# Low parts of later weights behind each head's products of scores and decay, in the recurrent stage of a two-layer hybrid model

## The chip, the cores and the metric

The kernel runs on one core of one Trainium2 chip. The metric is device time in microseconds (us) of one execution: 1385.5 us as the median of three runs of the kernel before (1385.12 to 1385.57). The engines are TensorE (PE in the profile, with PEld for its weight loads), VectorE (DVE), ScalarE (ACT), GpSimd (POOL) and SyncE (SP), which issues most loads.

## What is computed

512 tokens of width 1024 go through an attention layer, a SwiGLU, a recurrent (mLSTM) layer and a second SwiGLU, each with a norm and a residual sum. The change lies in the recurrent layer:

```
def mlstm_mixer(xn, w_in, conv_w, conv_b, ig_bias, fg_bias, head_gain, w_out):
    proj = xn @ w_in
    qk = silu(causal_depthwise_conv(proj[..., :2 * QK_WIDTH], conv_w, conv_b))
    v, o_pre, gates = ...
    ig = gates[..., :MLSTM_HEADS] + ig_bias
    lf = log_sigmoid(gates[..., MLSTM_HEADS:] + fg_bias)
    h = mlstm_chunkwise(q, k, vh, ig, lf)
    h = h * rsqrt(mean(h * h, axis=-1, keepdims=True) + RMS_EPS)
    return (h * head_gain * sigmoid(o_pre)) @ w_out
```

Per head the recurrence amounts to a causal product: scores q k^T, multiplied element by element with a decay matrix exp(b_t - b_s + ig_s - m_t), the result times the values (numerators), and a quotient. There are 8 heads with 64 channels of q and k and 128 of v.

## The kernel before

**Split products.** TensorE multiplies in a rounded format. So every weight chunk (128 partitions by 1024 elements) is split in two: a high part, cast on ScalarE (L223), and a low part, the difference between the raw chunk and the high part, on VectorE (L225). Activations are split the same way. Each product is three matmuls: high weight by high activation, high weight by low activation, low weight by high activation (`multiply`, L255). In `project_tokens` (L309), where the activations are the stationary operand, the low weight comes second. Raw chunks are loaded by SyncE's queue into three buffers in turn; high and low parts have three buffers each as well.

**Chunks and ticks.** The recurrent stage projects in this order: values of heads 0 to 3, then columns of q and k and values in blocks of 256: mqk0, mqk2, mv2, mqk1, mqk3, mv3, and the output gate mo0 to mo3. Each block has two chunks. A chunk is written as: load and split of this chunk (`split_chunk`), its matmuls for two output blocks of four times three each, then `advance()`, which counts a tick and writes out the work deferred to that tick. mv2 has ticks 9 and 10, mqk1 11 and 12, mqk3 13 and 14, mv3 15 and 16, mo0 17 and 18, mo1 19 and 20, mo2 21 and 22.

**The heads.** For each head three functions are deferred to ticks given in HEAD_AT: `decay`, `scores` and `numerators`. For heads 0 to 7 the scores stand at ticks 10, 11, 13, 14, 16, 17, 19, 20.

- `decay(hh)`: one matmul broadcasts the gate row of the head into a PSUM bank (nb, L2098), VectorE adds the causal mask (L2100), ScalarE writes exponentials into four tiles e (L2105, L2108). These tiles have two buffers, so those of head h wait until the numerators of head h - 2 have been read.
- `scores(hh)`: for each of four key blocks two matmuls write a bank (L2118, L2119; two banks in turn), and one product on VectorE multiplies scores and decay into e (L2120), 512, 384, 256 and 128 columns wide.
- `numerators(hh)`: 20 matmuls (L2130) into two banks, which are then read for the denominator (L2139 to L2142), for the sum of squares on ScalarE (L2145), for a Newton root (L189 to L194) and for the scaled output (L2152). The next head's numerators need those banks. Outputs go through memory by GpSimd's queue or, for the last two heads, through TensorE.

`stack(p)` (L2083 to L2089) prepares q and k of two heads out of the convolved blocks; `convolve` (L1939 to L1943) makes these from mqk.

**What sets the order.** Instructions are written in the order above, and each engine runs its own list in a fixed order. The lists are made when the program is built: an instruction may move ahead of ones written earlier when its operands are ready sooner. Two hooks hold it back. `tc.issue_after(ins)` puts what is written inside it behind `ins` on the engine of `ins`, in order only, without a wait of its own. `behind_scores()` in `split_chunk` does this to low parts, behind the instruction kept in `ahead_of_splits[0]`; `behind_factors()` does it to the high parts, by `ahead_of_casts[0]`. The attention stage sets both; at L1338, after it, both are set to None, and in the recurrent stage nothing sets them.

## Time and profile before

| | |
|---|---|
| median of 3 runs | 1385.5 us |
| the profiled execution, its own time | 1385.26 us |
| its span | 1383.5 us |
| TensorE busy in the span | 1368.5 us |
| VectorE busy in the span | 1111.3 us |
| TensorE busy in 870 to 990 us, the heads | 117.86 of 120 us |
| VectorE busy in 870 to 990 us | 102.98 of 120 us |
| ScalarE busy in 870 to 990 us | 83.28 of 120 us |
| low parts (L225) on VectorE in 870 to 990 us | 16, 19.41 us |
| products of scores and decay (L2120) there | 32, 15.13 us |

A row of a timeline gives start, duration, engine, line, operation, what is written and read, shape and count, and in brackets the idle time of the engine before it with what ended that. A row of waits gives the waiter, who released it, the total in us, the times and the longest. A row of windows gives, for a stretch, its length and the busy time of each engine with its number of instructions, then the granted clock and the load on the DMA engines.

### The profile page before, as it was taken

The numbers are of one execution on the slowest core, as the hardware profiler recorded it, in microseconds if no ns is written. First come the engines' busy times: TensorE is split into PE (matmuls) and PEld (weight loads), VectorE is DVE, ScalarE is ACT, GpSimd is POOL, SyncE is SP. The second block draws the span as 40 slices with busy tenths as digits, with TensorE's granted clock in tenths as the row PEclk, the third lists the DMA queues.
The fourth block names the chain that finished last, engine by engine and source line by source line (L and its number), as shares of the span: only waits on it lengthen the run. The fifth ranks groups of instructions, "written<-read, shape, count | busy, mean of one in ns | idle before, by whom it ended". The sixth has DMA issues, their size and how long they took to land. (4 is left out here: it accounts for less than half of the span.)

```text
span 1383.5 us, 22546 instructions
## 1 busy us (share of the span) xinstructions
PE 1368.5 (99%) x8740; PEld 1242.9 (90%) x8740; DVE 1111.3 (80%) x1845; ACT 780.5 (56%) x1246; POOL 180.2 (13%) x264
## 2 busy tenths in 40 slices
PE   9999999999999999999999999999999999999997
PEld 7888889899998889999999998898888999999886
DVE  7758769696896489788778798898858988887887
ACT  6556565656554354444476464695534454448854
POOL 3000013121211010000010110122102330001113
PEclk9999999999999999999999999999999999999999
DMA  8534255637286256323362742324335553335863
GB/s 298 176 120 139 77 153 161 197 122 237 91 280 205 102 137 183 111 73 122 122 153 77 168 124 80 103 66 119 92 122 124 156 173 105 122 122 129 192 167 100
DMA packets 140067, 193.81 MB, mean 140 GB/s; under 512 B 8980, under 2 KB 104788, under 8 KB 139960
## 3 DMA queue, kind: packets, MB, share of 16 engines
q1 hardware_dynamic: 119552, 139.81, 31.7%
q0 software_dynamic: 18752, 51.43, 15.7%
q8 instruction: 69, 1.13, 0.3%
q10 hardware_dynamic: 1656, 1.12, 0.2%
q14 instruction: 38, 0.31, 0.1%
HBM read 167.30 MB, written 22.54 MB: 137 GB/s over the span
## 5 line engine op out<-in xcount | busy, mean ns | idle before, releaser
L1696 POOL DMA_DIRECT2D f1T<-in_ffn_w_out_dram x15 | 17.8, 1185 | 208.7 <-DMA f1P_2w_w<-in_ffn_w_out_dram 135.7
L1671 POOL DMA_DIRECT2D f0S<-in_ffn_w_out_dram x10 | 8.7, 874 | 260.3 <-DVE f0hid L1588 173.1
L2228 POOL DMA_DIRECT2D hD<-hB x32 | 21.7, 697 | 68.3 <-DVE hB L2225 68.3
L255 PE MATMUL mo<-n_h,mo_k_l 128*128 128x512 f32 x64 | 25.3, 396 | 0.0
L255 PE MATMUL mo<-n_h,mo_k_h 128*128 128x512 f32 x64 | 25.3, 395 | 0.0
L255 PE MATMUL mo<-n_l,mo_k_h 128*128 128x512 f32 x64 | 25.2, 393 | 0.0
L255 PE MATMUL awo<-ao_h,awo_k_h 128*128 128x512 f32 x64 | 25.2, 393 | 0.0
L255 PE MATMUL mqk<-n_h,mqk_k_h 128*128 128x512 f32 x64 | 25.1, 392 | 0.0
L255 PE MATMUL mwo<-yo_l,mwo_k_h 128*128 128x512 f32 x64 | 25.1, 392 | 0.0
L255 PE MATMUL mqk<-n_l,mqk_k_h 128*128 128x512 f32 x64 | 25.1, 392 | 0.0
L255 PE MATMUL f0j<-n_h,f0j_h 128*128 128x512 f32 x64 | 25.0, 391 | 0.0
L255 PE MATMUL f1j<-n_h,f1j_h 128*128 128x512 f32 x64 | 25.0, 391 | 0.0
L255 PE MATMUL awo<-ao_h,awo_k_l 128*128 128x512 f32 x64 | 25.0, 391 | 0.0
L255 PE MATMUL mwo<-yo_h,mwo_k_l 128*128 128x512 f32 x64 | 25.0, 391 | 0.0
L255 PE MATMUL mqk<-n_h,mqk_k_l 128*128 128x512 f32 x64 | 25.0, 390 | 0.0
L255 PE MATMUL awo<-ao_l,awo_k_h 128*128 128x512 f32 x64 | 25.0, 390 | 0.0
L255 PE MATMUL f0j<-n_h,f0j_l 128*128 128x512 f32 x64 | 24.9, 390 | 0.0
L255 PE MATMUL f1j<-n_h,f1j_l 128*128 128x512 f32 x64 | 24.9, 390 | 0.0
L255 PE MATMUL f0j<-n_l,f0j_h 128*128 128x512 f32 x64 | 24.9, 389 | 0.0
L255 PE MATMUL f1j<-n_l,f1j_h 128*128 128x512 f32 x64 | 24.9, 389 | 0.0
L255 PE MATMUL mwo<-yo_h,mwo_k_h 128*128 128x512 f32 x64 | 24.8, 391 | 0.0
L225 DVE TENSOR_TENSOR v1P_l<-v1W,v1P_h 128x1024 fp32r<-128x1024 f32 x14 | 17.1, 1222 | 9.3 <-ACT v1P_h L223 9.3
(2613 smaller groups left out, 5875.7 us busy)
## 6 DMA issues: line engine op xcount, KB each, us to landing
f0j_w<-in_ffn_w_in_dram SPq DMA_DIRECT2D x17, 512.0 KB, 4.8
f1j_w<-in_ffn_w_in_dram SPq DMA_DIRECT2D x17, 512.0 KB, 6.4
f1T<-in_ffn_w_out_dram POOLq DMA_DIRECT2D x15, 512.0 KB, 7.0
f0hid<-in_ffn_w_in_dram SPq DMA_DIRECT2D x9, 512.0 KB, 5.2
f1hid<-in_ffn_w_in_dram SPq DMA_DIRECT2D x9, 512.0 KB, 4.8
v0W<-in_attn_w_in_dram SPq DMA_DIRECT2D x8, 512.0 KB, 6.1
v1W<-in_attn_w_in_dram SPq DMA_DIRECT2D x8, 512.0 KB, 3.5
awo_k_w<-in_attn_w_out_dram SPq DMA_DIRECT2D x8, 512.0 KB, 4.5
```

Source lines behind the costliest of these rows:

```text
L225: nc.vector.tensor_tensor(lo[:, :n], raw[:, :n], hi[:, :n].bitcast(F32), op=ALU.subtract)
L255: nc.tensor.matmul(acc, whl[a][:, k, m * P:(m + 1) * P], pairs[b][kk], start=(kk == 0 and (a, b) == SPLITS[0]), stop=(kk == nk - 1 and (a, ...
L1671: nc.gpsimd.dma_start(t, src[1][:, ks], accum_op=ALU.add)
L1696: nc.gpsimd.dma_start(view(to), weight_rows(hk * UNITS + u, n), accum_op=ALU.add)
L2228: nc.gpsimd.dma_start(hD[k // 4].rearrange("(b i) x -> i b x", i=R)[:, :, c0:c0 + R], t[R * a_:R * (a_ + 1)])
```

## The change

One line is added in `scores`, after the loop over the four key blocks:

```
                 nc.vector.scalar_tensor_tensor(e, sp[:, :w], 0.125, e, op0=ALU.mult, op1=ALU.mult)
+            ahead_of_splits[0] = last_on(DVE) if hh < H - 1 else None
```

`last_on(DVE)` is the last VectorE instruction written so far, here the fourth product of head hh. From then on every low part written in `split_chunk` stands behind that product in VectorE's list, until the scores of the next head put their own fourth product there; the scores of head 7 take the hook away again. So the chunks written after ticks 10 to 19 are concerned: both of mqk1, mqk3, mv3, mo0 and mo1, ten low parts. High parts, loads and everything on the other engines keep their rules.

## The prediction, made before the changed kernel was run

> **What bounds the kernel now.** I read the page first, for the engine that has no room.

> ```profile
> PE 1368.5 (99%) x8740; PEld 1242.9 (90%) x8740; DVE 1111.3 (80%) x1845; ACT 780.5 (56%) x1246; POOL 180.2 (13%) x264
> PEclk9999999999999999999999999999999999999999
> ```

> TensorE is busy for 1368.5 of 1383.5 us, at a granted clock in the top tenth in every slice. A reordering on VectorE (DVE) can win only what TensorE now waits, and loses whatever new wait it makes. So the second view is TensorE's waits in the stretch of the recurrent heads, 870 to 990 us.

> ```profile
> PE m4s L2118 <- DVE m4e L2120: 0.9, 1, 0.9
> PE m6yT L351 <- DVE m6yt L2152: 0.5, 1, 0.5
> PE m1nb L2098 <- ACT m0e L2108: 0.4, 1, 0.4
> PE m6num L2130 <- DVE m5yt L2152: 0.2, 1, 0.2
> ```

> Together 2.0 us: the most that this stage can give back. The third view cuts the stretch into windows, the busy time of PE, PEld, DVE, ACT and POOL.

> ```profile
> 890.00:910.00 20.00, 20.00 (x104) 16.79 (x103) 16.20 (x39) 13.96 (x34) 1.07 (x1) 1.00 0.27 80
> 910.00:930.00 20.00, 20.00 (x149) 18.98 (x148) 19.43 (x54) 19.36 (x41) 6.45 (x8) 1.00 0.32 79
> 930.00:950.00 20.00, 18.98 (x105) 15.53 (x104) 16.78 (x56) 13.23 (x43) 7.00 (x10) 1.00 0.46 119
> ```

> From 910 to 930 VectorE has 0.57 us of 20 to spare; at 890 to 910 it has 3.8. Then the timeline of VectorE, for the low parts (L225) and each head's last products (L2120).

> ```profile
> 877.19 1.21 DVE L225 TENSOR_TENSOR mqk_k_l<-mqk_k_w,mqk_k_h 128x1024 fp32r<-128x1024 f32 x1
> ...
> 884.36 1.22 DVE L225 TENSOR_TENSOR mqk_k_l<-mqk_k_w,mqk_k_h 128x1024 fp32r<-128x1024 f32 x1
> 885.50 1.15 DVE L2120 SCALAR_TENSOR_TENSOR m0e<-m0s,m0e 128x512 f32<-128x512 f32 x2
> ...
> 887.19 0.69 DVE L2120 SCALAR_TENSOR_TENSOR m0e<-m0s,m0e 128x256 f32<-128x256 f32 x2
> ...
> 892.91 1.16 DVE L2120 SCALAR_TENSOR_TENSOR m1e<-m1s,m1e 128x512 f32<-128x512 f32 x2 [2.34 <-PE m1s L2119]
> 893.98 1.22 DVE L225 TENSOR_TENSOR mqk_k_l<-mqk_k_w,mqk_k_h 128x1024 fp32r<-128x1024 f32 x1
> 895.11 0.61 DVE L2120 SCALAR_TENSOR_TENSOR m1e<-m1s,m1e 128x256 f32<-128x256 f32 x2
> ...
> 910.15 0.28 DVE L2120 SCALAR_TENSOR_TENSOR m2e<-m2s,m2e 128x128 f32<-128x128 f32 x1
> ...
> 920.12 0.28 DVE L2120 SCALAR_TENSOR_TENSOR m3e<-m3s,m3e 128x128 f32<-128x128 f32 x1
> ...
> 932.09 2.36 DVE L225 TENSOR_TENSOR mo_k_l<-mo_k_w,mo_k_h 128x1024 fp32r<-128x1024 f32 x2
> ...
> 938.74 0.29 DVE L2120 SCALAR_TENSOR_TENSOR m4e<-m4s,m4e 128x128 f32<-128x128 f32 x1
> ...
> 947.38 0.28 DVE L2120 SCALAR_TENSOR_TENSOR m5e<-m5s,m5e 128x128 f32<-128x128 f32 x1
> ...
> 960.97 0.28 DVE L2120 SCALAR_TENSOR_TENSOR m6e<-m6s,m6e 128x128 f32<-128x128 f32 x1
> ```

> The low part at 877.19 belongs to the chunk that the source writes behind head 0's products, and runs 8 us ahead of them: the order on an engine is set by readiness, and low parts run early.

> **The change, part by part.** It adds and removes no instruction. It orders each low part written after head h's products behind the last of them, for h = 0 to 6. The source goes in ticks, one weight chunk each: scores of heads 0 to 6 stand at ticks 10, 11, 13, 14, 16, 17, 19, so the chunk multiplied right after each is the first of mqk1, the second of mqk1, the second of mqk3, the first of mv3, both of mo0, the second of mo1. Three more low parts (first of mqk3, second of mv3, first of mo1) have a whole chunk between products and use, and cost the path nothing: chunks take 5.5 us of TensorE (the x24 row below) against 1.22 for one low part; without that cover each would cost up to 1.22.

> For the seven the next row decides: where TensorE first needs the low part.

> ```profile
> 886.92 0.39 PE L255 MATMUL mqk<-n_h,mqk_k_l 128*128 128x512 f32 x1
> ...
> 892.18 0.39 PE L2118 MATMUL m1s<-qs,ks 128*128 128x512 f32 x1
> ...
> 893.46 0.39 PE L255 MATMUL mqk<-n_h,mqk_k_l 128*128 128x512 f32 x1
> 893.69 0.35 PE L2118 MATMUL m1s<-qs,ks 128*128 128x256 f32 x1
> 893.88 0.28 PE L2119 MATMUL m1s<-ql,ks 128*128 128x256 f32 x1
> 894.00 0.40 PE L255 MATMUL mqk<-n_h,mqk_k_h 128*128 128x512 f32 x1
> ...
> 908.27 0.39 PE L255 MATMUL mqk<-n_h,mqk_k_l 128*128 128x512 f32 x1
> ...
> 917.24 0.28 PE L309 MATMUL mv<-mv_k_l,n_h 128*128 128x256 f32 x1
> ...
> 933.05 0.40 PE L255 MATMUL mo<-n_h,mo_k_l 128*128 128x512 f32 x1
> ...
> 943.94 0.40 PE L255 MATMUL mo<-n_h,mo_k_l 128*128 128x512 f32 x1
> ...
> 958.91 0.39 PE L255 MATMUL mo<-n_h,mo_k_l 128*128 128x512 f32 x1
> ```

> In every one the first use comes before the head's last product has ended. With nothing else shifted, the low part would be late by (end of last product) + 1.22 - (first use): head 0 887.88 + 1.22 - 886.92 = 2.2; head 1 895.72: 3.5; head 2 910.43: 3.4; head 3 920.40: 4.4; head 4 939.03: 7.2; head 5 947.66: 4.9; head 6 961.25: 3.6. TensorE's queue goes on meanwhile with what needs no low part. Its price is in the chain of waits:

> ```profile
> 899.18 2.23 PE m0num L2130 x20
> ...
> 901.64 5.50 PE mqk L255 x24
> ```

> 5.50/24 = 0.23 a matmul. The other half of the chunk (its second output block) has two ready matmuls (0.46; on mv3 one, half as wide: 0.12), the third and fourth score blocks follow (893.69 to 894.00 above is 0.3, the fourth is half as wide: 0.45 for both), and in heads 2, 4 and 6 the next head's gate broadcast (one matmul, 0.23). In head 0 the third block and the broadcast already stand ahead of the first use. So the cover is 0.6, 0.9, 1.1, 0.6, 1.1, 0.9, 1.1, and the **upper end** is 1.6 + 2.6 + 2.3 + 3.8 + 6.1 + 4.0 + 2.5 = 22.9, less the waits at m1nb and m4s that vanish (1.3): +21.6.

> The **lower end** takes away every delay of the products. In head 1 they are unhindered: scores start at 892.18, the first product at 892.91, and the four take 1.16 + 0.61 = 1.77 back to back. The low part is ready 0.73 + 1.77 + 1.22 = 3.7 after the scores start; TensorE has two score blocks (0.8, 892.18 to 892.99), its two opening matmuls (0.46; mv3 0.12) and what covers, head 0's third block and broadcast included: 2.1 to 2.4 (head 3: 1.5). Direct loss: 1.3 in heads 0, 2, 4, 6, 1.6 in heads 1 and 5, 2.2 in head 3: 10.6. Off it come head 0's bridge by head 1's first scores (0.8; their operands are ready by then) and head 1's by head 0's numerators (2.23, ready since 888: all 1.6), and the 1.3 of today's waits: +6.9. I take two thirds of a bridge by head 1's numerators in head 2 as well (-0.9): today they come just behind it, when a bank is free.

> ```profile
> L2130 PE MATMUL m1num<-vaug,m1e x20: 271/275/275, 911.3 to 913.4; 128*128 128x129 f32 x20
> ```

> That leaves 6.0.

> Between 6.0 and 21.6 I choose by what still delays the products. The low parts at 884.36 and 932.09 (3.6 us in all) step out from before products, and each loss gives the other engines slack, so I stay near the lower end. What remains: head 3's products share VectorE with the convolution of mqk3 in a window without room (+1.2, one low part); head 4's wait for exponentials that cannot start before head 2's numerators have freed their buffer (+1.5 of the 6.1 - 1.3 = 4.8 difference); head 5 the same way (+0.7); head 2 a mask addition and Newton steps (+0.5). 6.0 + 3.9 = **+10**. No load gets late: a raw chunk lands in 4 us and its buffer is wanted three chunks (16 us) on.

> ```profile
> mo_k_w<-in_mlstm_w_in_dram SPq DMA_DIRECT2D x8, 512.0 KB, 3.7
> ```

> Held up on VectorE behind a low part that waits: only small steps of the head before, which feed numerators a chunk later. After the stage TensorE is the bound again, so nothing is earned back. The profiled execution took 1385.26 (span 1383.5, 1.8 around it); 1385.3 + 10 = 1395.3. The median of the runs is 0.2 above it: **1395.5 us**.

> [...] The longest TensorE wait of this trace is 1.5 us, at the very start, and the ten matmuls behind it run slowly:

> ```profile
> 1.51 3.97 PE L108 MATMUL idle<-idle_w,ones_r 128*128 128x512 f32 x10 [1.51 <-DVE idle_w L103]
> ```

> That is 0.39 a matmul against 0.23 later, 1.6 us more for ten. [...]

> **The rivals.** (1) *TensorE bridges the gaps*: numerators (2.23 each) and next scores are pulled into every gap where they exist. For it: head 1's and head 0's are ready. Against: in heads 3 to 6 they are written earlier and wait for a bank, and run as soon as one is free. Left are heads 3 and 4 at their direct loss, 2.2 + 1.3 - 1.3: +2.2, 1387.7. (2) *Backlog*: low parts leave VectorE's empty 2.3 us at 890 for the full window, convolutions and stacks fall behind too, and the upper end comes true: +16 to +21.6, up to 1407. For it the 19.43 of 20; against it the slack that each loss makes. (3) *Not slower*: the products decide. Freed of the low parts at 884.36 and 932.09 they run up to 1.2 and 2.4 earlier, and all four waits (2.0) go; this holds if scores are pulled forward by 1.5 us or more, so that low parts still land before their first use: 1383.5. Against: scores stand in TensorE's full queue behind the chunk before. (4) *The clock drops*, as a mechanism here: if heads 3 and 4 leave one unbroken wait each as long as the start, twenty matmuls run at 0.39: +3.2 on the forecast, 1398.7. [...] (5) *No effect*: the products already precede. Only 910 to 947 could allow it, and four of the seven lie outside or show the contrary: 1385.5.

> **How the numbers follow.** Forecast 0.55 (its own range 1391 to 1400), (1) 0.14, (2) 0.16, (3) 0.08, (4) 0.04, (5) 0.03. A measurement tells 0.2% (2.8 us) from no change: slower is above 1388.3. Slower gets 0.55 + 0.16 + 0.04 + over half of (1) = 0.83; same the rest of (1), half of (3) and (5) = 0.13; faster half of (3), 0.04, since the stage's 2.0 us alone do not reach it. The range holds the forecast, (1), (4) and most of (2): 1387.4 to 1404.5.

> **What would show it.** After: TensorE's waits gain lines "mqk", "mv" and "mo" released by low parts (L225), 1 to 3 us each, seven at most, the longest at mv3 or mo0; m4s's and m1nb's lines shrink; each of the seven low parts starts within 0.3 us of its head's last product; VectorE's busy time in the stage stays. Wrong if those lines sum below 4 us, if the loss lies after 1000 us, or if matmuls behind a wait take 0.39 each from start to start.

## The result, and the profile after

The changed kernel takes 1399.07 us, the median of 4 runs (1398.94 to 1401.23), against 1385.45 before (4 runs): 13.6 us more, ratio 1.0101 with a 95% interval of 1.0088 to 1.0113. Forecast were 1395.5 us, in a range of 1387.4 to 1404.5. The profiled execution has a span of 1397.4 us.

The page of the changed kernel first: engines, then the granted clock in 40 slices.

```profile
PE 1375.8 (98%) x8740; PEld 1247.5 (89%) x8740; DVE 1111.8 (80%) x1845; ACT 778.0 (56%) x1244; POOL 178.1 (13%) x264
PEclk9999999999999999999999999999999999999999
```

VectorE works as long as before (1111.8 against 1111.3) and TensorE has the same 8740 matmuls, but is busy 7.3 us longer. The same work taking longer is the first sign that not only waiting was added; the slices are 35 us wide and too coarse to show why. TensorE's waits between 870 and 990 us (waiter, releaser, total, times, longest):

```profile
PE m4s L2118 <- DVE m4e L2120: 3.4, 1, 3.4
PE mv L309 <- DVE mv_k_l L225: 2.9, 1, 2.9
PE m3s L2118 <- DVE m3e L2120: 1.5, 2, 1.0
PE mqk L255 <- DVE mqk_k_l L225: 0.6, 1, 0.6
PE m6num L2131 <- DVE m5yt L2153: 0.3, 1, 0.3
PE m5num L2131 <- DVE m4yt L2153: 0.3, 1, 0.3
PE mo L255 <- DVE mo_k_l L225: 0.2, 1, 0.2
```

9.2 us where 2.0 stood. Three lines carry a low part (L225) as releaser, and two the products of heads 3 and 4. The windows of the same stretch, to be read against those of the prediction:

```profile
890.00:910.00 20.00, 20.00 (x98) 16.52 (x97) 15.48 (x38) 11.23 (x32) 0.00 (x0) 1.00 0.27 80
910.00:930.00 20.00, 14.99 (x81) 12.51 (x81) 19.22 (x53) 15.67 (x34) 5.49 (x8) 0.83 0.32 79
930.00:950.00 20.00, 16.37 (x107) 14.32 (x106) 10.60 (x32) 10.74 (x28) 4.12 (x6) 0.89 0.21 52
```

Up to 910 nothing is lost. Then TensorE falls to 15.0 and 16.4 of 20, and the column behind POOL, the granted clock, to 0.83 and 0.89: in these windows it runs slowly as well as standing. Before, it was 1.00 in all three. The two places lie at head 3 and head 4. First VectorE around them, each head's last product and the low part that now stands behind it:

```profile
922.10 0.28 DVE L2120 SCALAR_TENSOR_TENSOR m3e<-m3s,m3e 128x128 f32<-128x128 f32 x1
...
923.57 1.22 DVE L225 TENSOR_TENSOR mv_k_l<-mv_k_w,mv_k_h 128x1024 fp32r<-128x1024 f32 x1
...
947.50 0.28 DVE L2120 SCALAR_TENSOR_TENSOR m4e<-m4s,m4e 128x128 f32<-128x128 f32 x1
947.70 0.15 DVE L192 SCALAR_TENSOR_TENSOR m2rq_a<-m2rq_y 128x4 f32<-128x4 f32 x1
947.77 1.22 DVE L225 TENSOR_TENSOR mo_k_l<-mo_k_w,mo_k_h 128x1024 fp32r<-128x1024 f32 x1
```

Then TensorE at the first of them:

```profile
921.58 0.40 PE L255 MATMUL mo<-n_l,mo_k_h 128*128 128x512 f32 x1
924.84 0.58 PE L309 MATMUL mv<-mv_k_l,n_h 128*128 128x256 f32 x1 [2.87 <-DVE mv_k_l L225]
925.22 0.41 PE L309 MATMUL mv<-mv_k_h,n_l 128*128 128x256 f32 x1
925.43 0.41 PE L309 MATMUL mv<-mv_k_h,n_h 128*128 128x256 f32 x1
...
928.63 0.32 PE L309 MATMUL mv<-mv_k_h,n_h 128*128 128x256 f32 x1
928.79 0.28 PE L309 MATMUL mv<-mv_k_l,n_h 128*128 128x256 f32 x1
928.91 0.28 PE L309 MATMUL mv<-mv_k_h,n_l 128*128 128x256 f32 x1
```

Compare the starts and not the durations: out of the wait the matmuls follow each other every 0.21 us, and from 928.79 every 0.12: 3.8 us at about half speed. At the second place, behind the wait of 3.4, it is 0.43 instead of 0.23:

```profile
949.64 0.63 PE L255 MATMUL mo<-n_h,mo_k_h 128*128 128x512 f32 x1
950.07 0.63 PE L255 MATMUL mo<-n_l,mo_k_h 128*128 128x512 f32 x1
```

Nothing of the loss comes or goes later. The same matmuls of the last layer start, first and last, in the kernel before at

```profile
L2275 PE MATMUL finc<-f1P_0w_h,f1P x16: 389/389/396, 1267.8 to 1286.6; 128*128 128x512 f32 x16
```

and in the changed one 14.0 later:

```profile
L2276 PE MATMUL finc<-f1P_0w_h,f1P x16: 389/389/396, 1281.8 to 1300.6; 128*128 128x512 f32 x16
```

### The profile page after: what moved, and what is told of

Its sections match the earlier page's. It is cut to its first block, busy times and chain, and to the rows that moved or that the text cites. A ratio compares the mean times of both kernels' runs of the same rounds, so it can differ in the third digit from the quotient of the medians.

```text
span 1397.4 us, 22532 instructions
## 1 busy us (share of the span) xinstructions
PE 1375.8 (98%) x8740; PEld 1247.5 (89%) x8740; DVE 1111.8 (80%) x1845; ACT 778.0 (56%) x1244; POOL 178.1 (13%) x264
## 3 DMA queue, kind: packets, MB, share of 16 engines
q0 software_dynamic: 18752, 51.43, 15.5%
## 4 chain that ended last, share of the span: by engine, by line
PE 80%; DVE 11%; ACT 4%; issue 2%; DMA 1%; POOL 0%; ACTq 0%; DVEq 0%
PE fo L1864 8%; PE f1j_u L1549 6%; PE f0j_u L1549 6%; PE f1j_c L1549 4%; PE f1j_p L1549 4%; PE f0j_p L1549 4%; PE f0j_c L1549 4%; PE awo L255 3%; PE f0j L255 3%; PE f1j L255 3%; PE mwo L255 3%; PE mqk L255 2%; PE finc L2276 2%; PE mv L309 2%; PE finp L2276 2%
## 5 line engine op out<-in xcount | busy, mean ns | idle before, releaser
L255 PE MATMUL mo<-n_h,mo_k_h 128*128 128x512 f32 x64 | 25.9, 404 | 0.0
L255 PE MATMUL mo<-n_h,mo_k_l 128*128 128x512 f32 x64 | 25.6, 408 | 0.2 <-DVE mo_k_l L225 0.2
L255 PE MATMUL mo<-n_l,mo_k_h 128*128 128x512 f32 x64 | 25.6, 400 | 0.0
L255 PE MATMUL mqk<-n_h,mqk_k_l 128*128 128x512 f32 x64 | 24.9, 396 | 0.6 <-DVE mqk_k_l L225 0.6
L255 PE MATMUL awo<-ao_h,awo_k_h 128*128 128x512 f32 x64 | 25.2, 393 | 0.0
L255 PE MATMUL mqk<-n_l,mqk_k_h 128*128 128x512 f32 x64 | 25.1, 392 | 0.0
L255 PE MATMUL mqk<-n_h,mqk_k_h 128*128 128x512 f32 x64 | 25.0, 391 | 0.0
L255 PE MATMUL f1j<-n_h,f1j_h 128*128 128x512 f32 x64 | 25.0, 391 | 0.0
L255 PE MATMUL f0j<-n_h,f0j_h 128*128 128x512 f32 x64 | 25.0, 391 | 0.0
L255 PE MATMUL awo<-ao_h,awo_k_l 128*128 128x512 f32 x64 | 25.0, 391 | 0.0
L255 PE MATMUL mwo<-yo_h,mwo_k_l 128*128 128x512 f32 x64 | 25.0, 391 | 0.0
L255 PE MATMUL mwo<-yo_l,mwo_k_h 128*128 128x512 f32 x64 | 25.0, 391 | 0.0
L255 PE MATMUL mwo<-yo_h,mwo_k_h 128*128 128x512 f32 x64 | 25.0, 390 | 0.0
L255 PE MATMUL awo<-ao_l,awo_k_h 128*128 128x512 f32 x64 | 25.0, 390 | 0.0
L255 PE MATMUL f0j<-n_h,f0j_l 128*128 128x512 f32 x64 | 24.9, 390 | 0.0
L255 PE MATMUL f1j<-n_h,f1j_l 128*128 128x512 f32 x64 | 24.9, 390 | 0.0
L255 PE MATMUL f0j<-n_l,f0j_h 128*128 128x512 f32 x64 | 24.9, 389 | 0.0
L255 PE MATMUL f1j<-n_l,f1j_h 128*128 128x512 f32 x64 | 24.9, 389 | 0.0
L225 DVE TENSOR_TENSOR v1P_l<-v1W,v1P_h 128x1024 fp32r<-128x1024 f32 x14 | 17.1, 1224 | 9.3 <-ACT v1P_h L223 9.3
## 6 DMA issues: line engine op xcount, KB each, us to landing
f0j_w<-in_ffn_w_in_dram SPq DMA_DIRECT2D x17, 512.0 KB, 4.7
f1j_w<-in_ffn_w_in_dram SPq DMA_DIRECT2D x17, 512.0 KB, 5.9
f1T<-in_ffn_w_out_dram POOLq DMA_DIRECT2D x15, 512.0 KB, 7.1
f0hid<-in_ffn_w_in_dram SPq DMA_DIRECT2D x9, 512.0 KB, 6.1
f1hid<-in_ffn_w_in_dram SPq DMA_DIRECT2D x9, 512.0 KB, 5.1
v0W<-in_attn_w_in_dram SPq DMA_DIRECT2D x8, 512.0 KB, 7.1
v1W<-in_attn_w_in_dram SPq DMA_DIRECT2D x8, 512.0 KB, 3.8
awo_k_w<-in_attn_w_out_dram SPq DMA_DIRECT2D x8, 512.0 KB, 4.7
```

The source lines that it names most:

```text
L225: nc.vector.tensor_tensor(lo[:, :n], raw[:, :n], hi[:, :n].bitcast(F32), op=ALU.subtract)
L255: nc.tensor.matmul(acc, whl[a][:, k, m * P:(m + 1) * P], pairs[b][kk], start=(kk == 0 and (a, b) == SPLITS[0]), stop=(kk == nk - 1 and (a, ...
```

## The experiments

Three theories were put against each other. **A**: TensorE stands for a low part, or for products, in heads 3 and 4, and behind its long stands, 2.9 and 3.4 us in the changed kernel, runs at half clock. **B**: ten low parts moved into full windows set VectorE back as a whole. **C**: every head pays alike.

### Which heads pay

Four kernels, each with the hook for some of the heads only:

```
-            ahead_of_splits[0] = last_on(DVE) if hh < H - 1 else None
+            ahead_of_splits[0] = last_on(DVE) if hh < 3 else None
...
+            ahead_of_splits[0] = last_on(DVE) if hh == 3 else None
...
+            ahead_of_splits[0] = last_on(DVE) if hh == 4 else None
...
+            ahead_of_splits[0] = last_on(DVE) if 5 <= hh < H - 1 else None
```

> The hook is set by heads 0 to 2 only and taken away at head 3: five low parts are ordered (mqk1, mqk3, the first of mv3 not). Theory A (the loss is TensorE standing for a late low part in heads 3 and 4, and half clock after each stand): TensorE bridges heads 0 and 1, head 2 costs at most one wait of 0.6: 1385 to 1387 us. Theory B (backlog on VectorE out of all ten moved low parts): these five bring about half of the loss, 1391 to 1394, though no single wait is long. Theory C (every head pays alike): three sevenths, 1391.

> Only head 3 sets the hook: both low parts of mv3 are ordered. Theory A: the wait of mv for its low part (2.9) and the half clock behind it (18 matmuls at 0.21 instead of 0.12, 1.7) stay: 1389 to 1392, with the granted clock below 1 in one place. Theory B: two of ten low parts, 1387 to 1388, clock 1.00 throughout. Theory C: one seventh, 1387.4.

> Only head 4 sets the hook: the first low part of mo0 is ordered. [...] If the stand at m4s in the changed kernel came from the delay handed down by head 3 instead, 1386 to 1387. Theory B: one of ten, 1386 to 1387. Theory C: 1387.4.

> Only heads 5 and 6 set the hook: the second low part of mo0 and both of mo1. Theory A: no long wait, since the changed kernel shows 0.2 there: 1385 to 1387, clock 1.00. What I predicted (1 to 2 us per head): 1387 to 1389. Theory B: three of ten, 1388 to 1390. Theory C: 1389.

Measured beside a median of 1385.78 of the kernel before (27 runs on that chip): heads 0 to 2 1386.89, ratio 1.0008 (0.9999 to 1.0018); head 3 1390.54, 1.0034 (1.0023 to 1.0046); head 4 1389.67, 1.0026 (1.0016 to 1.0035); heads 5 and 6 1386.93, 1.0009 (0.9999 to 1.0018). So +1.1, +4.8, +3.9 and +1.2. The intervals of the first and the last touch 1, so these two are not shown to cost anything. The first kernel orders four low parts, both of mqk1 and both of mqk3, and not five as its expectation says. Theories B and C would have these four cost 5 us or more (four tenths or three sevenths of 13.6); they cost about 1. B's and C's prices for head 3, 1.6 to 2.5, are half of what two low parts cost there.

The kernel with head 4 alone shows the second place undisturbed. Its profiled execution is the fastest of its nine runs, 1387.30. TensorE's wait there:

```profile
PE m4s L2118 <- DVE m4e L2120: 1.9, 1, 1.9
```

It ends 0.4 later than the wait of 0.9 of the kernel before (936.13 against 935.77) and begins earlier by the three matmuls with the low part that used to run in front of it. What holds m4e's products is not the same in the two. In the kernel before, two other low parts stand in front of them on VectorE (932.09 to 934.45), while the exponentials run early:

```profile
932.97 0.87 ACT L2108 ACTIVATE m4e<-m4nb,bcol 128x128 f32<-128x128 f32 x3
```

With head 4 alone these two low parts run behind the products, but now ScalarE's list has head 2's sum of squares in front of the exponentials:

```profile
932.97 0.35 ACT L2146 ACTIVATE m2j<-m2num,m2rr 128x128 f32<-128x128 f32 x1
...
934.34 0.89 ACT L2108 ACTIVATE m4e<-m4nb,bcol 128x128 f32<-128x128 f32 x3
```

So the added line, which names VectorE alone, has also changed the order on ScalarE: the reciprocal that the sum of squares needs runs at 932.64 here, at 934.95 in the kernel before, and the lists are made by readiness. Then the clock, in windows of 1 us (PE's busy time is the first number behind the length; the clock is the third from the end):

```profile
936.00:937.00 1.00, 0.87 (x4) 0.62 (x5) 0.95 (x5) 0.87 (x4) 0.23 (x1) 1.00 0.00 0
937.00:938.00 1.00, 1.00 (x5) 0.54 (x3) 1.00 (x5) 0.00 (x0) 0.33 (x1) 0.69 0.00 0
938.00:939.00 1.00, 1.00 (x3) 0.50 (x2) 1.00 (x3) 0.00 (x0) 0.00 (x0) 0.50 0.66 254
939.00:940.00 1.00, 0.80 (x3) 0.52 (x3) 1.00 (x3) 0.00 (x0) 0.00 (x0) 0.50 0.05 16
940.00:941.00 1.00, 1.00 (x4) 0.82 (x3) 1.00 (x3) 0.00 (x0) 0.00 (x0) 0.60 0.43 33
941.00:942.00 1.00, 1.00 (x6) 0.79 (x6) 0.96 (x3) 0.00 (x0) 0.00 (x0) 1.00 0.98 332
```

By these windows the half clock comes 1.3 us after the wait has ended (937.4 against 936.13) and lasts 3.4 us, to 940.8. The nine runs of this kernel lie 4.6 us apart, and the mean granted clock goes with them in part: the three with 0.996 took 1390.0 to 1391.9, the two with 0.998 and 0.999 took 1387.9 and 1388.4, but the four with 0.997 took 1387.3 to 1390.1, the fastest run among them.

The four parts add to 11.0 of the 13.6. Whether the rest belongs to heads 3 and 4 together was asked with a fifth kernel (`hh in (3, 4)`):

> Heads 3 and 4 set the hook, the others not: both low parts of mv3 and the first of mo0 and no other are ordered. The four kernels with parts of the hook add to 1.1 + 4.8 + 3.9 + 1.2 = 11.0 over the kernel before, the whole change to 13.6. If the rest (2.6) comes from head 3's delay lengthening the stand at head 4 (3.4 in the whole change, 1.9 with head 4 alone): 4.8 + 3.9 + 2.6 = 11.3, 1397. If it comes from the other heads acting together: 8.7, 1394.4.

Measured: 1397.05 beside 1385.40, +11.7, ratio 1.0082 (1.0068 to 1.0096). The sum of its two parts is 8.7; the 3.0 on top, about 2.8 either way by the three intervals, come from the two together. Its trace shows where: its wait at m4s is 3.4, as in the whole change, against 1.9 with head 4 alone, and the mean granted clock of its profiled execution is 0.994, as in the whole change, against 0.997 with head 3 alone and with head 4 alone. With heads 0 to 2 and 5 and 6 (1.1 and 1.2) that makes 14.0 of 13.6: heads 3 and 4 carry nearly all of the change, and the rest is within what these medians tell.

### How much of it is the clock

If the clock falls because TensorE stands, work without use in the stands must make the kernel faster. The opening matmul of mo0 is repeated, each time starting its output block anew, so the sum is the same:

```
+            for _ in range(again if kk == 0 else 0):
+                nc.tensor.matmul(acc, whl[0][:, k, m * P:(m + 1) * P], pairs[0][kk], start=True, stop=True)
             for a, b in SPLITS:
...
-                    multiply(acc[m], whl, pairs, ch, m, nk)
+                    multiply(acc[m], whl, pairs, ch, m, nk, again=(11, 12)[m] if name == "mo0" else 0)
```

In TensorE's list nothing else moves: 11 repeats come in front of mv's first low-part matmul, 12 in front of m4s's third block. The same edit in the kernel before is the control.

> The changed kernel with the opening matmul of mo0 repeated, 11 times for its first and 12 times for its second output block; each repeat starts its block anew. In TensorE's list they stand in the two long stands (before mv's first low-part matmul, and before m4s's third block), 2.5 and 2.7 us of work at 0.23 each. Theory A (half of what is lost behind a stand is the clock, which falls because TensorE stands): the low parts land no sooner, but the matmuls behind run at 0.12 and 0.23 instead of 0.21 and 0.43, 1.7 and about 3 us: 1394 to 1395.5, granted clock 1.00 in every window. Rival (the slow pace has another cause, such as the reordering itself): 1399, with the same slow matmuls. Second rival (added work simply costs): 23 x 0.23 = 5.3 more, 1404.

> The same 23 repeats in the kernel before, where there is no long stand to put them in. Both theories: they cost their work less the wait of 0.9 at m4s that they fill, 4.3 to 5.3: 1390 to 1391, clock 1.00.

Measured beside 1385.40: the changed kernel with repeats 1395.79, ratio 1.0073 (1.0057 to 1.0088); the kernel before with repeats 1390.59, 1.0035 (1.0022 to 1.0047). The 23 matmuls cost 5.2 where there is no stand, and in the changed kernel they win 3.3. At the second place the repeats end the matter: the wait at m4s is down to 0.7,

```profile
PE m4s L2120 <- DVE m4e L2122: 0.7, 1, 0.7
```

and the clock stays whole:

```profile
944.00:946.00 2.00, 1.30 (x6) 0.66 (x5) 1.90 (x8) 1.93 (x8) 0.00 (x0) 1.00 0.00 0
946.00:948.00 2.00, 1.62 (x7) 0.78 (x5) 2.00 (x7) 0.00 (x0) 0.00 (x0) 1.00 0.00 0
948.00:950.00 2.00, 1.55 (x7) 1.30 (x8) 1.90 (x8) 0.00 (x0) 0.00 (x0) 1.00 0.21 20
```

Not so at the first, where my expectation of 1.00 in every window missed:

```profile
920.00:922.00 2.00, 1.29 (x6) 0.94 (x7) 2.00 (x9) 1.45 (x4) 0.34 (x1) 1.00 0.37 111
922.00:924.00 2.00, 2.00 (x7) 1.55 (x6) 2.00 (x9) 1.97 (x3) 0.00 (x0) 0.59 0.05 21
924.00:926.00 2.00, 2.00 (x7) 1.57 (x6) 2.00 (x7) 1.93 (x4) 0.00 (x0) 0.56 0.00 0
926.00:928.00 2.00, 2.00 (x17) 1.91 (x16) 1.97 (x6) 0.43 (x1) 0.00 (x0) 1.00 0.73 201
```

The clock had fallen before the repeats could prevent it, behind the two waits for head 3's products (1.0 and 0.5 us). The repeats ran slowly instead of mv's matmuls, took 4.2 us for 11 and held mv up until 926.34, 1.1 later than its low part needed (that starts at 924.00 here, 0.4 later than in the changed kernel); the mv matmuls behind them, up to the first of m4s, then took 5.8 instead of 7.5. So 3.3 us of the 13.6, about 2.8 either way by the intervals, are the half clock by these two times, and up to 4.4 if the 1.1 of overrun are counted. The 7.3 us that TensorE is busy longer in the changed kernel are more than that price: at head 4 the slow matmuls up to 949.04 run while the low part of mo is still missing, so at full speed TensorE would have waited instead.

### Cover instead of an earlier low part

The changed kernel keeps its hook, but each chunk of mqk, mv and mo first does all matmuls with the high part, 16 of 24, and then those with the low part:

```
+                        for part in ((0, 0), (0, 1)), ((1, 0),):
+                            for k, (u, v) in itertools.product(range(4), part):
+                                nc.tensor.matmul(acc[m], whl[u][:, k, m * P:(m + 1) * P], pairs[v][4 * ch + k],
+                                                 start=(ch == k == 0 and (u, v) == (0, 0)),
+                                                 stop=(ch == 1 and k == 3 and u == 1))
```

(and alike in `project_tokens`); the control has the same order without the hook.

> The changed kernel with another order of the matmuls in a chunk of mqk, mv and mo: first all that use the high part of the weights (16 of 24 per chunk, 32 of 48 on mv), then those with the low part. The low parts land as late as before. Theory A (TensorE stands because only the opening matmuls of a chunk can run without the low part): 3.7 us of work now cover each low part, the stands of 0.6, 2.9 and 0.2 for low parts go and with them the half clock; m4s keeps a wait of up to 0.9. 1385 to 1388. Theory of backlog (products and convolutions late by themselves): 1393 or more stays.

> The same order of matmuls in the kernel before, where low parts are never late. Theory A: nothing to cover, 1384.5 to 1386. It is there to tell what the new order does by itself.

Measured beside 1385.47: with the hook 1390.01, ratio 1.0036 (1.0023 to 1.0049); without it 1387.49, 1.0016 (1.0007 to 1.0025). Both came out above what I expected, because the new order costs 2.0 by itself, most of it at a place it does not aim at: the wait at m1nb in head 0, 0.4 before, is 1.8 without the hook. With the hook TensorE's waits begin with

```profile
PE m1nb L2105 <- ACT m0e L2115: 1.9, 1, 1.9
PE m5num L2138 <- DVE m4yt L2160: 1.2, 1, 1.2
PE mo L271 <- DVE mo_k_l L225: 0.6, 1, 0.6
```

Between the two kernels with this order the hook costs 2.5 us instead of 13.6. The waits for low parts on mqk and mv are gone, and so is the one at m4s; 0.6 is left on mo, and the granted clock is 1.00 over 870 to 990 us. So the low parts' lateness hurts by want of other work at the head of a chunk, as theory A has it. The numbers of this pair rest on 5 and 11 runs, and the 2.5 has about 2 either way by the intervals.

### Two ways to have the order without the stand

First, the hook is set one tick later, so that every low part has a chunk between the products and its use:

```
-            ahead_of_splits[0] = last_on(DVE) if hh < H - 1 else None
+            defer(1, lambda p=last_on(DVE) if hh < H - 1 else None: ahead_of_splits.__setitem__(0, p))
```

> The hook is set one tick later: the chunk written right after a head's scores keeps the hook of the head before, the next chunk gets this head's. Every low part then has a chunk of TensorE work (5.5 us) between the products and its first use. Theory A: no stand for a low part, and the low parts of mo0 and mo1 at 932 no longer stand before m4e's products: the waits of 0.9 and 0.4 of the kernel before shrink, 1384.5 to 1385.8. Theory of backlog on VectorE (all ten low parts moved out of idle time): 1388 to 1392.

Measured: 1385.80 beside 1385.40, ratio 1.0000 (0.9991 to 1.0009). Ten low parts stand behind products here too (mqk1's first is free, mo2's first is added), VectorE is as full as before at 910 to 930 (19.71 of 20), and they cost nothing: backlog is not it. But the gain that I allowed did not come either. The wait at m4s is gone and another stands before it:

```profile
PE m2num L2131 <- DVE m1yt L2153: 1.5, 1, 1.5
```

Second, the hook is set at head 4 alone, one tick later. The expectation counts three low parts behind it; the edit orders two, the second of mo0 and the first of mo1, since head 6's scores take the hook away before mo1's second chunk is written:

```
+            if hh == 4:
+                defer(1, lambda p=last_on(DVE): ahead_of_splits.__setitem__(0, p))
+            if hh == 6:
+                ahead_of_splits[0] = None
```

> The kernel before with the hook for three low parts only: the second of mo0 and both of mo1 stand behind head 4's last product, and have at least a chunk until they are used. The two that ran at 932 no longer delay m4e's products, for which TensorE waits 0.9 in the kernel before. If that wait was theirs: 1384.5 to 1385 (0.9 less at most). If m4e's products wait for the exponentials anyway: 1385.4, no change.

Measured: 1384.35 beside 1385.47, ratio 0.9992 (0.9983 to 1.0001). The wait at m4s is no longer among TensorE's waits of this kernel, which are now

```profile
PE m6yT L351 <- DVE m6yt L2156: 0.5, 1, 0.5
PE m1nb L2098 <- ACT m0e L2108: 0.4, 1, 0.4
PE m5num L2134 <- DVE m4yt L2156: 0.3, 1, 0.3
```

1.1 us less is what the vanished 0.9 would give, but the interval touches 1, so that it is faster is not shown. And the wait did not go because m4e's products come sooner: the first starts at 935.85 here, at 935.04 in the kernel before, again behind exponentials that follow head 2's sum of squares. TensorE's list has fifteen matmuls of mo in front of m4s's third block here, nine in the kernel before, and they fill the time.

## Why the prediction was right, point by point

The direction and the size were right: 1399.07 lies in the forecast's own range of 1391 to 1400. The sum behind it was right in part only, and that its total fits is partly luck. Of the three signs that the prediction named as showing it wrong, two came true: the lines released by low parts sum to 3.7 us (2.9 + 0.6 + 0.2), below 4, and matmuls behind a wait follow each other every 0.43 us, slower than the 0.39 that it named. The third, a loss after 1000 us, did not. The line at m4s, which was to shrink, grew from 0.9 to 3.4. The measured time is nearly that of rival (4), the clock, 1398.7, and the condition of that rival held: heads 3 and 4 leave one wait each that is longer than the 1.5 at the start.

- **The bound.** TensorE had 2.0 us to win in the stage and a full queue to lose; it lost, and nothing came back behind the stage (14.0 later at the last layer's first matmuls, 13.6 in the time). Right.
- **The mechanism.** Low parts that the source writes right after a head's scores land after TensorE wants them. Right for mqk, mv and mo, but they are the smaller part of the waits: 3.7 of the 9.2 us of waits are for low parts, 4.9 for the products of heads 3 and 4. The low parts start right behind the last product (0.27 us from start to start in head 4), in head 3 1.5 after it, and with other work to do in the meantime (the order with high parts first, or a hook one tick late) the loss falls to 2.5 or to nothing.
- **Heads 0 and 1**, direct losses of 1.3 and 1.6 less a bridge: bridged wholly, with head 0's numerators and head 1's scores. Head 2, taken at 0.9: a wait of 0.6.
- **Head 3**, 2.2 + 1.2 = 3.4: waits of 1.5 and 2.9, 4.4. The convolution did stand between, as the 1.2 had it: the low part starts 1.2 after the last product has ended.
- **Head 4**, 1.3 + 1.5 = 2.8, of which 0.9 were there before: the wait is 3.4, of which 1.5 only in the presence of head 3's delay (1.9 by itself). It is a wait for m4e's products, not for the low part: TensorE has run out of matmuls that need neither. I had priced that only as cover missing, and had the products run sooner once low parts leave VectorE; they did not, by the timelines because the exponentials moved behind head 2's sum of squares.
- **Heads 5 and 6**, 2.3 and 1.3: 0.2 and nothing in the whole change, +1.2 together when tried alone, which is not clear of noise. Numerators and the next head's scores are there to bridge: rival (1), which I had thought unlikely from head 3 on, holds for these two.
- **The clock** is the step that failed. I set it aside at 0.04, taking the length of one unbroken wait as what decides, which no run shows; nor is it shown that the ten slow matmuls at the start, by which I priced it, were a case of it: their pace is 0.39, but the granted clock reads 1.00 in the windows from 1.50 to 5.50. Here the clock fell after a wait of 1.9 (head 4 alone) and after two of 1.0 and 0.5 in a row (with repeats, and in the changed kernel itself, as shown below). The fall cost about 3.3 us, a quarter of the loss, so that my +10 for the stands alone agrees with the +10.4 of the kernel with repeats partly by luck: too much at heads 5 and 6, too little at 3 and 4.
- **Slack from the losses.** I stayed near the lower end because each loss gives the other engines time. That was right for heads 5 and 6. For head 4 it went the other way: head 3's delay lengthened its wait from 1.9 to 3.4. The timelines say how, though it was not tried by itself. From the start of head 2's numerators to m4s's third block it is 6.6 us with head 4 alone (929.55 to 936.13) and 6.8 in the whole change (938.72 to 945.47), so the products come hardly later by that count. What TensorE lacks in between is work: m4s's first two blocks (0.9) had already run before the numerators, and two of mo's six matmuls (0.46) in front of the stand on mv.

## What to carry to other kernels

An instruction that is put behind another engine's chain has to be traced to its first use: what lies between the two, in work of the engine that bounds the kernel, is the allowance, and where it is smaller than the chain's tail plus the instruction itself, the difference is paid in full unless that engine has other ready work. The same edge one weight chunk later cost nothing here (1385.80 beside 1385.40). And a wait on TensorE is to be priced with the slow matmuls that may follow it, not only with its own length: here 3.4 us at half clock followed one wait of 1.9 (head 4 alone) and two of 1.0 and 0.5 close to each other (with repeats), and none followed another wait of 1.9 (high parts first, with the hook).

## What the runs showed of the hardware that was not expected

```profile
918.46:921.88 3.42, 1.95 (x10) 0.97 (x8) 3.42 (x11) 2.89 (x8) 0.66 (x2) 1.00 0.26 77
921.88:925.29 3.41, 0.55 (x3) 0.45 (x3) 3.41 (x11) 3.34 (x5) 0.00 (x0) 0.50 0.00 0
925.29:928.70 3.41, 3.41 (x18) 3.41 (x18) 3.35 (x11) 0.69 (x2) 0.00 (x0) 0.50 0.55 154
928.70:932.12 3.42, 3.42 (x30) 3.42 (x30) 3.36 (x5) 1.98 (x3) 1.67 (x3) 1.00 0.14 24
...
942.36:945.77 3.41, 0.30 (x2) 0.30 (x2) 1.79 (x8) 3.41 (x17) 0.00 (x0) 1.00 0.00 0
945.77:949.18 3.41, 3.21 (x10) 1.90 (x8) 3.10 (x11) 0.46 (x2) 0.00 (x0) 0.50 0.00 0
```

The clock falls at 921.88 and at 945.77, seven steps apart, and comes back two steps after each fall. With head 3 alone, with head 4 alone and with repeats it falls once in this stage, for 3.4 us, one step. Each fall ends a step in which TensorE was busy for little: 1.95 and 0.30 us here, 1.35 with head 3 alone, 1.55 with head 4 alone, 1.96 with repeats. So it is not the wait of 2.9 that lowers the clock at head 3: the fall comes 0.1 us before that wait begins, behind the waits of 1.0 and 0.5. That wait leaves TensorE 0.55 us of work in the next step, and the clock stays down for a second; with the repeats in that step it came back after one. At head 4 this does not tell the two apart: the step behind the fall is busy for 3.21 us here and with head 4 alone, and the clock came back only after two steps here, after one there.

The length of a wait does not decide by itself. The clock fell after a single wait of 1.87 us (head 4 alone), and stayed at 1.00 after one of 1.90 (at m1nb, with high parts first and the hook), one of 1.8 (at m1nb, high parts first, no hook) and one of 1.5 (at m2num, later hook), while waits of 1.0 and 0.5 in one step were followed by a fall. Nor has a step to be without work for the clock to fall at its end: up to 1.96 us of it stood there. Where the limit lies is not shown.

The steps lie at other times after the start from trace to trace: the falls at 921.88 here and at 937.4 with head 4 alone are 15.5 us apart, four and a half steps. At head 3 the step from 925.29 to 928.70 is busy throughout, and the clock is 1.00 behind it. That a wait counts by where it falls in the steps would fit the nine runs of one kernel that differ by 4.6 us, but only one of these has a trace, so this is not shown.
